# Output projection of a hybrid conv/attention layer: block products reordered, gate columns stored, x reloaded into other tiles

## The chip, the core and the metric

The kernel runs on one core of one Trainium2 chip. The metric is the device time of one launch in microseconds (us), as the median of several runs. Before the change it is 1453.81 us (three runs, 1452.35 to 1453.82).

## The reference, cut to what matters

One layer over a sequence of 512 positions and 2048 channels, in float32:

```python
mod = silu(c) @ w_ada + b_ada                     # shift, scale, gate: 2048 columns each
h = rms_norm(x, g_pre) * (1 + scale) + shift
p = h @ w_in                                      # cv, cg, cz, q, k, v, az, m_conv, m_attn
y_conv = conv_branch(cv, cg, cz, ...)             # ... @ w_conv_out
y_attn = attn_branch(q, k, v, az, ...)            # ... @ w_attn_out
merged = sigmoid(m_conv) * y_conv + sigmoid(m_attn) * y_attn
out = merged @ w_o                                # 512x2048 by 2048x2048: the output projection
x = x + gate * rms_norm(out, g_post)
```

## The kernel before, in words

Every float32 operand of a large matmul is kept as a sum of two float32r parts, high and low (`split`, L143: ScalarE casts the high part, VectorE subtracts it from the source to get the low one). `mm3` (L165) then makes one product from three matmuls: high by high, high by low, low by high. Weights arrive by `wraw` (L153, one DMA into a tile with tag "wr", three buffers) and are split by `wsplit` (L158, tags "wh" and "wl", three buffers each). All DMAs are issued from SyncE's queue (SP).

The stages in order of time: x is normalised and the convolution's input products run (to about 350 us), then attention and the depthwise convolution, the gates cz, ma and mc of the branches, the two branch projections (`gemm_y`: "ya" from w_attn_out, then "yc" from w_conv_out), and the output projection. The code is written with a planner: instructions are traced in program order, and a list scheduler puts each on its engine's queue by its own estimate of when operands and buffers are ready, earlier code first among the ready ones. It can issue an instruction long before its place in the code when a buffer is free. A tile's buffer is given to any later tile of its tag once all readers of the old one are done. `ordered` (L678) keeps the matmuls of the late stages in program order.

Tile pools that matter here: pages (`page`, 27 of 128x512), pairs (`pair_of`, 16 of 128x2x512), temps (`temp`, 12 of 128x512 in the late stages), "ws" (two of 128x2x512).

**Output projection.** It is done by a scheme of seven block products in place of eight (Winograd's form of Strassen's): the merged operand is cut into blocks B11, B21, B22 and the sums T1 to T4 (L988 to L994; B11 and T1 lie in the merged pairs mB[0..7], T2 and T3 in the pages mT23, T4 in mT4), the weights into a11, a21, a12, a22 and the sums s1 = a21 + a22 (L1067), s2 = s1 + a11 (L1070), s3 = a11 + a21 (L1079, in place of a21) and s4 = s2 + a12 (L1104, L1116). `G` walks over two halves of the output columns. In each half the first loop (t = 0 to 3, two of eight weight row blocks each) makes four products per t, each of 12 matmuls (`oprod`, L1001): in this order ox (s2 by T2), oz (a11 by B11), or (s3 by T3), oy (s1 by T1). In ox's turn both s2 sums are needed, and they are temps. After t = 3, q = oz - ox, ct = or - q and ct - oy are formed (L1076, L1078, L1084, L1087). The second loop adds a12 by B21 into oz, a22 by T4 into or and s4 by B22 into oy. For G = 1 it is cut in two: first all s4 products (L1111 to L1117), then a third loop over t (L1123) with the a22 and a12 products. There t = 0 and 1 run at once, and t = 2 and 3 are split and held (L1130), then run for row tile i = 0 and i = 1 one after the other (L1139), so that row tile 0 can be finished under the products of row tile 1.

`out_done` (L1025) squares a finished output block on ScalarE and multiplies it by the gate columns `gg[n]` on VectorE; `finish` (L1044) makes the reciprocal root of the sum of squares, adds x (L1052) and stores a row tile. x is read again by `x_again` (L1039) into a 1 MB tile of tag "wr", the tag of the weights' raw tiles.

**Gate columns.** `gate(n)` (L802) computes one quarter of gate times g_post, as a row copied over all partitions: 16 loads of w_ada rows (temps "adag"), a running sum on VectorE (L820), one matmul with ones, and L830/L831. gate(0) to gate(2) are worked in between the mc products, gate(3) between the ya products; `pump` draws one step or a few at each product. The result of gate(0) lies in `dist`, those of 1 to 3 each in a page from then to the end of the kernel.

Of the kernel before, what the change touches and what calls it, by code (L numbers as in the profile page):

```python
# [51 lines left out]
def hybrid_trunk(ctx: ExitStack, tc: tile.TileContext, x, c, w_ada, b_ada, g_pre, g_post, w_in,  # L52
# [17 lines left out]
    def page(name, dt=F32):  # L70
        return pp.tile([P, S], dt, tag="pg", name=name)
# [730 lines left out]
    def gate(n):  # L802
# [21 lines left out]
        gp = page(f"gg_{n}") if n else dist  # L824
# [7 lines left out]
        gg[n] = gp  # L832
# [206 lines left out]
    def x_again(t):  # L1039
        xr = wp.tile([P, 4, 512], F32, tag="wr", name=f"xr_{t}")  # L1040
        nc.sync.dma_start(out=xr.rearrange("p k n -> p (k n)"), in_=x2[t * P:(t + 1) * P, :])
        return xr

    def finish(t, xr, cuts=((0, 4),)):  # L1044
        z = small(1, f"fz_{t}")
        nc.vector.scalar_tensor_tensor(z, fss[:, 4 * t + 3:4 * t + 4], 1.0 / D, fz[:, t:t + 1],
                                       op0=ALU.mult, op1=ALU.add)
        r = rsqrt1(z, f"fr_{t}")
        for a, b in cuts:
            for n in range(a, b):  # L1050
                g = xr[:, n, :]
                nc.vector.scalar_tensor_tensor(g, og[t][n], r, g, op0=ALU.mult, op1=ALU.add)  # L1052
            nc.sync.dma_start(out=out2[t * P:(t + 1) * P, a * 512:b * 512],
                              in_=xr[:, a:b, :].rearrange("p k n -> p (k n)"))

    work.append(late_splits())
    for G in range(2):
# [3 lines left out]
        for t in range(4):  # L1061
            ra = wraw(w_o[0], 2 * t, 2, c0, 1024, f"oa_{G}_{t}")
            s1 = mp.tile([P, 2, S], F32, tag="ws", bufs=2, name=f"os1_{G}_{t}")
            nc.sync.dma_start(out=s1, in_=w_o[0].rearrange("(t p) n -> p t n", p=P)[:, KH + 2 * t:KH + 2 * t + 2,
                                                                                  c0 + S:c0 + 2 * S])
            a11, a21 = ra[:, :, :S], ra[:, :, S:]
            nc.vector.tensor_tensor(s1, a21, s1, op=ALU.add)  # L1067
            for k in range(2):
                s2[2 * t + k] = temp(f"os2_{G}_{2 * t + k}")
                nc.vector.tensor_tensor(s2[2 * t + k], s1[:, k, :], a11[:, k, :], op=ALU.add)  # L1070
            oprod(ox, wop_of(s2[2 * t:2 * t + 2], f"os2_{G}_{t}"), oT2, t, True)
            oprod(oz, wop(a11, f"oa11_{G}_{t}"), oB11, t, True)
            if t == 3:
                q = [temp(f"oq_{G}_{i}") for i in range(2)]
                for i in range(2):
                    nc.scalar.copy(q[i], oz[i])  # L1076
                for i in range(2):
                    nc.vector.tensor_tensor(q[i], q[i], ox[i], op=ALU.subtract)  # L1078
            nc.vector.tensor_tensor(a21, a11, a21, op=ALU.add)  # L1079
            oprod(orr, wop(a21, f"os3_{G}_{t}"), oT3, t, True)  # L1080
            if t == 3:
                ct = [temp(f"oc_{G}_{i}") for i in range(2)]
                for i in range(2):
                    nc.vector.tensor_tensor(ct[i], orr[i], q[i], op=ALU.subtract)  # L1084
            oprod(oy, wop(s1, f"os1_{G}_{t}"), oT1, t, True)
# [25 lines left out]
        for t in range(4):  # L1111
# [5 lines left out]
            oprod(oy, wop_of(s2[2 * t:2 * t + 2], f"os4_{G}_{t}"), oB22, t, False)  # L1117
        for t in (2, 3, 0, 1):
            for n in range(2):
# [3 lines left out]
        for t in range(4):  # L1123
# [8 lines left out]
            if t == 0:  # L1132
                for i in range(2):
# [4 lines left out]
                    finish(2 + i, x_again(2 + i))  # L1138
        for i in range(2):  # L1139
            xr = x_again(i)  # L1140
# [9 lines left out]
            finish(i, xr, ((0, 2), (2, 3), (3, 4)) if i else ((0, 4),))  # L1150
# [29 lines left out]
```

## Time and profile before

| | |
|---|---|
| median of the runs | 1453.81 us (1452.35 to 1453.82) |
| the profiled execution's own time | 1453.56 us |
| its span, first to last instruction | 1451.6 us |
| TensorE matmul busy (PE) | 1387.0 us, 96% |
| TensorE weight load busy (PEld) | 1176.7 us, 81% |
| VectorE busy (DVE) | 1175.2 us, 81% |
| ScalarE busy (ACT) | 558.8 us, 38% |
| mean DMA rate | 172 GB/s |
| mean granted TensorE clock | 0.986 of full speed |

All times of the trace are us from the start of its span. In a row of the timeline the first number is the start, the second the duration; in square brackets stands how long the engine was idle before the instruction, and what ended that. Matmuls are pipelined: a row shows 0.39 us for a 512-column matmul where the next one starts 0.227 us later, so a busy PE is not a PE at its peak; a product's length is best read from the starts of two successive products. SPq rows are the issue of a DMA; the data lands later. "PEclk" is the granted clock, 1.00 being 2.4 GHz.

### The profile page before, as it was taken

What the parts mean: (1) busy time and instruction counts of PE and PEld (TensorE: products, weight loads), DVE (VectorE), ACT (ScalarE), POOL (GpSimd) and SP (SyncE); (2) the same over time, 40 slices, a digit from 0 to 9 for tenths busy, and PEclk for the clock granted to TensorE, in tenths of its full rate; (3) what the DMA queues carried; (4) which work ended last, traced back from release to release, by engine and by line L of the source; (5) the groups of instructions that cost most, each with busy time, mean ns of one, the idle gap of its engine ahead of it and who ended that gap; (6) DMA issues with size and microseconds to landing.
All of it is one profiled execution on the core that took longest, in us unless ns stands there. A gap on an engine that the chain in (4) does not pass through costs nothing.

```text
span 1451.6 us, 20533 instructions
## 1 busy us (share of the span) xinstructions
PE 1387.0 (96%) x7903; PEld 1176.7 (81%) x7903; DVE 1175.2 (81%) x1916; ACT 558.8 (38%) x903; POOL 1.8 (0%) x8
## 2 busy tenths in 40 slices
PE   5999999999999999999999999999998999799995
PEld 4676788887778777789999999999986888688774
DVE  6997976988888886698987888899877758888786
ACT  3422232223443244444544444444436223344441
POOL 0000000000000000000000000000000000000000
PEclk9999999999999999999999999999999999999997
DMA  9888633332223223244645565666689633235455
GB/s 305 292 274 296 229 120 116 117 102 81 93 66 102 95 73 101 68 143 159 204 138 186 175 192 189 205 208 227 210 297 335 235 130 135 94 131 174 137 200 228
DMA packets 180323, 249.11 MB, mean 172 GB/s; under 512 B 9649, under 2 KB 120578, under 8 KB 179330
## 3 DMA queue, kind: packets, MB, share of 16 engines
q1 hardware_dynamic: 180226, 247.80, 51.2%
q8 instruction: 62, 1.02, 0.3%
q14 instruction: 35, 0.29, 0.1%
HBM read 218.41 MB, written 29.36 MB: 171 GB/s over the span
## 4 chain that ended last, share of the span: by engine, by line
PE 83%; DVE 9%; DMA 4%; ACT 1%; issue 1%; SPq 1%; DVEq 0%; ACTq 0%
PE pc L167 10%; PE pg_k L167 6%; PE py_yc L167 6%; PE pv L167 6%; PE py_ya L167 5%; PE pg_az L167 5%; PE pg_q L167 5%; PE x_ma L167 5%; PE x_mc L167 4%; PE z_ma L167 3%; PE y_ma L167 3%; PE y_mc L167 3%; PE z_mc L167 3%; PE x_cz L167 2%; PE oy L167 2%; PE oz L167 2%
## 5 line engine op out<-in xcount | busy, mean ns | idle before, releaser
L500 DVE SCALAR_TENSOR_TENSOR cacc<-u,cw,cacc 128x511 f32<-128x511 f32 (+14 forms) x240 | 164.3, 728 | 0.0
L167 PE MATMUL pc<-hp,wh_c 128*128 128x512 f32 x512 | 160.3, 398 | 2.6 <-DVE part L369 1.2
L167 PEld LDWEIGHTS pc<-hp,wh_c 128*128 128x128 f32 x512 | 95.9, 190 | 28.8 <-issue 2.7
L167 PE MATMUL pc<-hp,wl_c 128*128 128x512 f32 x256 | 99.2, 397 | 2.1 <-DVE wl_c L146 2.1
L167 PE MATMUL py_ya<-ya,wh_ya 128*128 128x512 f32 x256 | 80.5, 396 | 8.3 <-ACT wh_ya L145 8.3
L369 DVE TENSOR_TENSOR part<-pc,part 128x512 f32<-128x512 f32 x96 | 64.7, 687 | 24.1 <-PE pc L167 23.6
L167 PE MATMUL pv<-wh_v,hp 128*128 128x512 f32 x256 | 82.9, 397 | 0.9 <-DVE part L369 0.9
L167 PE MATMUL pg_q<-hp,wh_q 128*128 128x512 f32 x256 | 82.6, 398 | 0.0
L167 PE MATMUL pg_az<-hp,wh_az 128*128 128x512 f32 x256 | 81.4, 395 | 0.0
L167 PE MATMUL pg_k<-hp,wh_k 128*128 128x512 f32 x256 | 80.0, 392 | 0.0
L145 ACT CAST wh_c<-wr_c 128x1024 fp32r<-128x1024 f32 (+1 forms) x36 | 34.2, 956 | 103.7 <-DMA wr_c<-in_w_in_dram 49.7
L167 PEld LDWEIGHTS py_ya<-ya,wh_ya 128*128 128x128 f32 x256 | 48.8, 191 | 19.2 <-ACT wh_ya L145 8.7
L167 PEld LDWEIGHTS pc<-hp,wl_c 128*128 128x128 f32 x256 | 48.6, 191 | 14.1 <-DVE wl_c L146 3.3
L167 PEld LDWEIGHTS pv<-wh_v,hp 128*128 128x128 f32 x256 | 47.8, 188 | 14.3 <-issue 4.5
L167 PEld LDWEIGHTS pg_az<-hp,wh_az 128*128 128x128 f32 x256 | 47.7, 188 | 12.0 <-issue 2.7
L167 PEld LDWEIGHTS pg_q<-hp,wh_q 128*128 128x128 f32 x256 | 47.2, 188 | 12.3 <-issue 2.8
L167 PEld LDWEIGHTS pg_k<-hp,wh_k 128*128 128x128 f32 x256 | 47.9, 188 | 9.4
L307 DVE SCALAR_TENSOR_TENSOR acc<-ada,cact,acc 128x512 f32<-128x512 f32 (+1 forms) x52 | 50.5, 970 | 1.6 <-DMA ada<-in_w_ada_dram 1.4
L167 PE MATMUL pg_k<-hp,wl_k 128*128 128x512 f32 x128 | 51.0, 399 | 0.0
L167 PE MATMUL pv<-wl_v,hp 128*128 128x512 f32 x128 | 50.6, 395 | 0.0
L167 PE MATMUL pg_az<-hp,wl_az 128*128 128x512 f32 x128 | 50.5, 396 | 0.0
L167 PE MATMUL py_ya<-ya,wl_ya 128*128 128x512 f32 x128 | 50.5, 394 | 0.0
(399 smaller groups left out, 3944.1 us busy)
## 6 DMA issues: line engine op xcount, KB each, us to landing
ada<-in_w_ada_dram SPq DMA_DIRECT2D x128, 256.0 KB, 5.4
wr_ma<-in_w_in_dram SPq DMA_DIRECT2D x16, 1024.0 KB, 5.7
wr_mc<-in_w_in_dram SPq DMA_DIRECT2D x16, 1024.0 KB, 5.5
adag<-in_w_ada_dram SPq DMA_DIRECT2D x64, 256.0 KB, 5.7
wr_c<-in_w_in_dram SPq DMA_DIRECT2D x28, 512.0 KB, 6.0
wr_v<-in_w_in_dram SPq DMA_DIRECT2D x8, 1024.0 KB, 5.3
wr_q<-in_w_in_dram SPq DMA_DIRECT2D x8, 1024.0 KB, 5.1
wr_k<-in_w_in_dram SPq DMA_DIRECT2D x8, 1024.0 KB, 6.2
```

The costliest lines, as they stand in the source:

```text
L145: nc.scalar.copy(hi, src)
L167: mm = nc.tensor.matmul(ps, a[p], b[q], start=start and i == 0, stop=stop and i == 2, skip_group_check=more)
L307: nc.vector.scalar_tensor_tensor(acc, raw[:, kk - k0, :, :], cact[:, kk:kk + 1], acc, op0=ALU.mult, op1=ALU.add)
L369: nc.vector.tensor_tensor(part[i], ps[f], part[i], op=ALU.add)
L500: paced(nc.vector.scalar_tensor_tensor(cvo[t][:, s:], u[t][:, :S - s], wj, cvo[t][:, s:], op0=ALU.mult, op1=ALU.add))
```

## The change

Three things change. In `gate`, the columns for n = 1 to 3 are computed in a temp instead of a page and stored to DRAM scratch; ahead of the output projection three pages are allocated and the columns fetched back. `x_again` loads a row tile of x as two halves of 512 KB into two tiles of the pairs' pool instead of one 1 MB tile of tag "wr"; it is called for all four row tiles ahead of the third loop of G = 1, and `finish` stores each of them in halves (for row tile 1 as before, a half and two quarters). In the first loop of each G the order of the four products becomes oz, or, ox, oy (and for the very first t oz, oy, or, ox), with the sums moved to where they are first used; the sums after t = 3 stand in the function of the ox product.

```diff
--- before.py
+++ after.py
@@ -821,7 +821,7 @@
             yield
         bg = temp(f"bg_{n}")
         nc.sync.dma_start(out=bg, in_=b_ada2[2 * D + n * 512:2 * D + (n + 1) * 512].partition_broadcast(P))
-        gp = page(f"gg_{n}") if n else dist
+        gp = temp(f"gg_{n}") if n else dist
         nc.sync.dma_start(out=gp, in_=g_post[0][n * 512:(n + 1) * 512].partition_broadcast(P))
         yield
         pgt = gbank(f"pgt_{n}", "t")
@@ -829,7 +829,10 @@
         yield
         nc.vector.tensor_tensor(bg, pgt, bg, op=ALU.add)
         nc.vector.tensor_tensor(gp, gp, bg, op=ALU.mult)
-        gg[n] = gp
+        if n:
+            spill(f"gg{n}", gp)
+        else:
+            gg[0] = gp
         yield
 
     crs = []
@@ -1037,23 +1040,29 @@
         nc.vector.tensor_scalar(fz[:, t:t + 1], fz[:, t:t + 1], 1.0 / D, 4.0 * EPS, op0=ALU.mult, op1=ALU.add)
 
     def x_again(t):
-        xr = wp.tile([P, 4, 512], F32, tag="wr", name=f"xr_{t}")
-        nc.sync.dma_start(out=xr.rearrange("p k n -> p (k n)"), in_=x2[t * P:(t + 1) * P, :])
+        xr = []
+        for a in range(2):
+            xr.append(pair_of(f"xr_{t}_{a}", F32))
+            nc.sync.dma_start(out=xr[a].rearrange("p k n -> p (k n)"),
+                              in_=x2[t * P:(t + 1) * P, a * 1024:(a + 1) * 1024])
         return xr
 
-    def finish(t, xr, cuts=((0, 4),)):
+    def finish(t, xr, cuts=((0, 2), (2, 4))):
         z = small(1, f"fz_{t}")
         nc.vector.scalar_tensor_tensor(z, fss[:, 4 * t + 3:4 * t + 4], 1.0 / D, fz[:, t:t + 1],
                                        op0=ALU.mult, op1=ALU.add)
         r = rsqrt1(z, f"fr_{t}")
         for a, b in cuts:
             for n in range(a, b):
-                g = xr[:, n, :]
+                g = xr[n // 2][:, n % 2, :]
                 nc.vector.scalar_tensor_tensor(g, og[t][n], r, g, op0=ALU.mult, op1=ALU.add)
             nc.sync.dma_start(out=out2[t * P:(t + 1) * P, a * 512:b * 512],
-                              in_=xr[:, a:b, :].rearrange("p k n -> p (k n)"))
+                              in_=xr[a // 2][:, a % 2:a % 2 + b - a, :].rearrange("p k n -> p (k n)"))
 
     work.append(late_splits())
+    for n in range(1, 4):
+        gg[n] = page(f"gg_{n}")
+        fetch(f"gg{n}", gg[n])
     for G in range(2):
         c0 = G * 1024
         s2 = [None] * KH
@@ -1064,25 +1073,46 @@
             nc.sync.dma_start(out=s1, in_=w_o[0].rearrange("(t p) n -> p t n", p=P)[:, KH + 2 * t:KH + 2 * t + 2,
                                                                                   c0 + S:c0 + 2 * S])
             a11, a21 = ra[:, :, :S], ra[:, :, S:]
-            nc.vector.tensor_tensor(s1, a21, s1, op=ALU.add)
-            for k in range(2):
-                s2[2 * t + k] = temp(f"os2_{G}_{2 * t + k}")
-                nc.vector.tensor_tensor(s2[2 * t + k], s1[:, k, :], a11[:, k, :], op=ALU.add)
-            oprod(ox, wop_of(s2[2 * t:2 * t + 2], f"os2_{G}_{t}"), oT2, t, True)
-            oprod(oz, wop(a11, f"oa11_{G}_{t}"), oB11, t, True)
-            if t == 3:
-                q = [temp(f"oq_{G}_{i}") for i in range(2)]
-                for i in range(2):
-                    nc.scalar.copy(q[i], oz[i])
-                for i in range(2):
-                    nc.vector.tensor_tensor(q[i], q[i], ox[i], op=ALU.subtract)
-            nc.vector.tensor_tensor(a21, a11, a21, op=ALU.add)
-            oprod(orr, wop(a21, f"os3_{G}_{t}"), oT3, t, True)
-            if t == 3:
-                ct = [temp(f"oc_{G}_{i}") for i in range(2)]
-                for i in range(2):
-                    nc.vector.tensor_tensor(ct[i], orr[i], q[i], op=ALU.subtract)
-            oprod(oy, wop(s1, f"os1_{G}_{t}"), oT1, t, True)
+
+            def p1():
+                oprod(oz, wop(a11, f"oa11_{G}_{t}"), oB11, t, True)
+                if t == 3:
+                    for i in range(2):
+                        q[i] = temp(f"oq_{G}_{i}")
+                        nc.scalar.copy(q[i], oz[i])
+
+            def p5():
+                oprod(oy, wop(s1, f"os1_{G}_{t}"), oT1, t, True)
+
+            def p6():
+                for k in range(2):
+                    s2[2 * t + k] = temp(f"os2_{G}_{2 * t + k}")
+                    nc.vector.tensor_tensor(s2[2 * t + k], s1[:, k, :], a11[:, k, :], op=ALU.add)
+                oprod(ox, wop_of(s2[2 * t:2 * t + 2], f"os2_{G}_{t}"), oT2, t, True)
+                if t == 3:
+                    for i in range(2):
+                        nc.vector.tensor_tensor(q[i], q[i], ox[i], op=ALU.subtract)
+                    for i in range(2):
+                        ct[i] = temp(f"oc_{G}_{i}")
+                        nc.vector.tensor_tensor(ct[i], orr[i], q[i], op=ALU.subtract)
+
+            def p7():
+                nc.vector.tensor_tensor(s3, a11, a21, op=ALU.add)
+                oprod(orr, wop(s3, f"os3_{G}_{t}"), oT3, t, True)
+
+            q, ct, s3 = [None] * 2, [None] * 2, a21
+            if G == 0 and t == 0:
+                p1()
+                nc.vector.tensor_tensor(s1, a21, s1, op=ALU.add)
+                p5()
+                p7()
+                p6()
+            else:
+                p1()
+                nc.vector.tensor_tensor(s1, a21, s1, op=ALU.add)
+                p7()
+                p6()
+                p5()
         for i in range(2):
             nc.vector.tensor_tensor(ct[i], ct[i], oy[i], op=ALU.subtract)
             out_done(2 * G + 1, 2 + i, ct[i], ct[i], tmp(f"osq22_{G}_{i}"))
@@ -1115,7 +1145,9 @@
             for k in range(2):
                 nc.vector.tensor_tensor(s2[2 * t + k], s2[2 * t + k], a12[:, k, :], op=ALU.add)
             oprod(oy, wop_of(s2[2 * t:2 * t + 2], f"os4_{G}_{t}"), oB22, t, False)
+        xrs = [None] * NT
         for t in (2, 3, 0, 1):
+            xrs[t] = x_again(t)
             for n in range(2):
                 og[t][n] = page(f"ogf_{n}_{t}")
                 fetch(f"og_{n}_{t}", og[t][n])
@@ -1135,9 +1167,9 @@
                     nc.vector.tensor_tensor(g, oy[i], q[i], op=ALU.add)
                     out_done(2, 2 + i, g, g, temp(f"osq12_{G}_{i}"))
                     sums3(2 + i)
-                    finish(2 + i, x_again(2 + i))
+                    finish(2 + i, xrs[2 + i])
         for i in range(2):
-            xr = x_again(i)
+            xr = xrs[i]
             for t, w in held:
                 oprod(orr, w[0], oT4, t, False, (i,))
             g = temp(f"oc21_{G}_{i}")
@@ -1147,7 +1179,7 @@
             for t, w in held:
                 oprod(oz, w[1], oB21, t, False, (i,))
             out_done(2, i, oz[i], temp(f"oc11_{G}_{i}"), temp(f"osq11_{G}_{i}"))
-            finish(i, xr, ((0, 2), (2, 3), (3, 4)) if i else ((0, 4),))
+            finish(i, xr, ((0, 2), (2, 3), (3, 4)) if i else ((0, 2), (2, 4)))
 
 
 # ---- launch: one core; inputs and outputs as the reference has them ----
```

## Rows read from the trace of the kernel before

**Rows 1.** The page: busy time of each engine, its share, and instructions.

```profile
PE 1387.0 (96%) x7903; PEld 1176.7 (81%) x7903; DVE 1175.2 (81%) x1916; ACT 558.8 (38%) x903; POOL 1.8 (0%) x8
```

**Rows 2.** Busy time by stretch: length, PE, PEld, DVE, ACT, POOL, granted clock, DMA share, GB/s.

```profile
907.00:1074.00 167.00, 165.87 (x1371) 164.61 (x1370) 148.58 (x181) 72.49 (x91) 0.00 (x0) 1.00 0.66 219
...
1260.40:1268.10 7.70, 0.18 (x1) 0.00 (x0) 7.56 (x16) 3.13 (x6) 0.00 (x0) 0.81 0.00 0
1268.10:1281.50 13.40, 13.09 (x49) 10.38 (x50) 12.08 (x16) 7.71 (x11) 0.00 (x0) 0.85 0.36 117
1281.50:1346.60 65.10, 65.10 (x288) 53.70 (x286) 51.67 (x63) 28.81 (x42) 0.00 (x0) 1.00 0.45 155
1346.60:1354.90 8.30, 5.01 (x14) 3.74 (x14) 7.96 (x12) 4.28 (x8) 0.00 (x0) 0.79 0.41 131
...
1407.20:1440.40 33.20, 26.73 (x97) 19.81 (x96) 23.20 (x61) 9.85 (x21) 0.00 (x0) 0.90 0.59 222
1440.40:1451.60 11.20, 0.00 (x0) 0.00 (x0) 6.69 (x20) 0.67 (x2) 0.00 (x0) 0.60 0.48 187
```

**Rows 3.** Waits of TensorE from 1262 us on: total, times, longest.

```profile
PE ox L167 <- ACT wh_os L145: 9.6, 2, 7.5
...
PE or L167 <- ACT wh_oa L145: 3.3, 2, 3.0
```

**Rows 4.** Chain that ended last: a product of the output projection.

```profile
1281.46 2.72 PE ox L167 x12
```

**Rows 5.** Timeline around the start of the output projection.

```profile
1250.88 0.62 ACT L145 CAST mt23h<-mt 128x512 fp32r<-128x512 f32 x1 [4.28 <-PE py_yc L167]
...
1266.66 1.28 DVE L1070 TENSOR_TENSOR os<-os,wr_oa 128x512 f32<-128x512 f32 x2
1267.44 0.62 ACT L145 CAST wh_os<-os 128x512 fp32r<-128x512 f32 x1 [0.92 <-DVE os L1070]
...
1268.11 0.80 PE L167 MATMUL ox<-wh_os,mt23h 128*128 128x512 f32 x1 [7.52 <-ACT wh_os L145]
```

**Rows 6.** Timeline around the start of the second column half (G = 1).

```profile
1347.39 0.68 DVE L1070 TENSOR_TENSOR os<-os,wr_oa 128x512 f32<-128x512 f32 x1
...
1350.40 1.22 DVE L146 TENSOR_TENSOR wl_oa<-wr_oa,wh_oa 128x1024 fp32r<-128x1024 f32 x1
```

**Rows 7.** SP's queue and ScalarE, late in G = 1: loads of x and of raw weights.

```profile
1376.86 0.34 SPq L1041 DMA_DIRECT2D xr<-in_x_dram  x1
...
1407.13 0.38 SPq L155 DMA_DIRECT2D wr_ob<-in_w_o_dram  x1
...
1412.13 2.00 ACT L145 CAST wh_oa<-wr_ob 128x1024 fp32r<-128x1024 f32 x2 [3.06 <-DMA wr_ob<-in_w_o_dram]
1422.73 2.19 ACT L145 CAST wph_oa<-wr_ob 128x512 fp32r<-128x512 f32 x4 [8.60 <-DMA wr_ob<-in_w_o_dram]
1427.84 2.18 ACT L145 CAST wh_oa<-wr_ob 128x512 fp32r<-128x512 f32 x4 [2.92 <-DMA wr_ob<-in_w_o_dram]
```

**Rows 8.** VectorE: the finishing of row tiles 2 and 3, and the last one.

```profile
1411.57 1.41 DVE L1052 SCALAR_TENSOR_TENSOR xr<-ogf,fr_y,xr 128x512 f32<-128x512 f32 x2
...
1446.00 1.41 DVE L1052 SCALAR_TENSOR_TENSOR xr<-oc,fr_y,xr 128x512 f32<-128x512 f32 x2
```

**Rows 9.** Gate columns: their tile's rows, a later bias load, and loads of w_ada.

```profile
L825 SPq DMA_DIRECT2D gg<-in_g_post_dram x3: 328/382/572, 752.5 to 1137.9; - x3
L831 DVE TENSOR_TENSOR gg<-gg,bg x3: 682/691/691, 1027.2 to 1175.4; 128x512 f32<-128x512 f32 x3
...
1014.86 0.42 SPq L823 DMA_DIRECT2D bg<-in_b_ada_dram  x1
...
1039.47 3.12 SPq L809 DMA_DIRECT2D adag<-in_w_ada_dram  x4
```

**Rows 10.** DMA issues of the late stages: size and median us to landing.

```profile
xr<-in_x_dram SPq DMA_DIRECT2D x4, 1024.0 KB, 4.8
...
os<-in_w_o_dram SPq DMA_DIRECT2D x6, 512.0 KB, 3.8
```

## The prediction

> **What bounds the kernel now.** I read the page first: TensorE (PE) is busy 96% of the span, VectorE (DVE) 81% [rows 1], so what can be won lies where PE stands still or is slow. Next the busy time by stretch [rows 2]: from 907 to 1074 us PE is busy 165.87 of 167 us, but from 1260.4 us, where the branch projections end, three stretches stand out. In 1260.4 to 1268.1 PE does nothing, in 1346.6 to 1354.9 it is busy 5.0 of 8.3 us, in 1407.2 to 1440.4 it is busy 26.7 of 33.2, and in each the granted clock falls to between 0.79 and 0.90. The waits of PE name the culprits [rows 3]: ox on the cast of os (9.6 us), or on the cast of oa (3.3 us). What a product costs when nothing is late is read from the chain of waits: 2.72 us for its 12 matmuls [rows 4].
>
> The timeline tells why. At the start, ox is the first product, and its operand s2 is made at 1266.66 and cast at 1267.44 [rows 5]. DVE was busy 7.56 of the 7.7 us before [rows 2] with the last merged blocks, whose temps s2 also needs. ScalarE (ACT) meanwhile had idled 4.28 us before 1250.88 [rows 5]: a11 could have been cast then. At the start of G = 1 it is the same, s2 at 1347.39 [rows 6]. In the third loop it is another thing: the raw weights come late. x is loaded at 1376.86 into a tile of their tag, the next raw weights are issued only at 1407.13, and ACT waits 3.06, 8.60 and 2.92 us for such loads [rows 7].
>
> **The change, part by part.** A DVE subtraction over 128x1024 takes 1.22 us [rows 6], two over 128x512 1.28 us [rows 5].
>
> **A, the first t.** From the end of the branch projections at 1260.4 to t = 1 at 1281.46 [rows 2, 4] go 21.1 us; four products are 4 x 2.72 = 10.9, so 10.2 us are lost. After the change oz (a11 by B11) and oy (s1 by T1) come first; both need only weights and merged blocks made long before, so their splits can lie under the last branch projections, where ACT and DVE have gaps. They cover PE until 1260.4 + 5.4 = 1265.8. The third, or, takes a split buffer that the last branch projection holds to its end, so its low part stands behind DVE's chain, which ends at 1266.66 [rows 5]; with 1.22 us for it and 0.64 for one late split of T2/T3 it is there at 1268.5. So 2.7 us are lost still, and **7.5 us** gained. Bounds: 10.2 if DVE slips that split into its chain; 4.9 if it puts the s2 sums and their split (2 x 1.28) ahead.
>
> **B, the start of G = 1.** ox takes 8.3 us for 2.72 [rows 2]: 5.6 lost. Now oz leads, with a11 loaded and no temp needed, and or follows without one either; s2 is wanted 5.4 us later. But DVE is full there (7.96 of 8.3 us [rows 2]) with the outputs of G = 0, so I leave one subtraction, 1.2 us, and 0.4 for slow matmuls after it: 1.6 lost, **4.0 us** gained. Bounds: 5.6; and 2.8, if both first subtractions (2 x 1.22) stay uncovered.
>
> **C, the third loop.** Eight products are 21.8 us of the 33.2 [rows 2, 4]: 11.4 lost. x no longer stands in the weights' tag; its halves go into pairs mB[0..7], the first of which die after oy of t = 0 of G = 1, near 1354.9 + 3 x 2.72 = 1363 [rows 2, 4], far ahead of their use at 1411.57 [rows 8]. If such a load stands at the head of SP's queue before its pair is dead, the weights behind it wait too; they have a whole t, 10.9 us, to spare. So all raw weights of the third loop but the last can be there before 1407. Then DVE decides: it still has 23.20 + 6.69 = 29.9 us to do from 1407.2 to the end [rows 2]; it ended at 1447.4 [rows 8] and can't end before 1437.1, so at most 10.3 us come of the 11.4. The finishing of row tiles 2 and 3 stands ahead of the later splits in the code; it costs PE part of this. I take 2.4 us for two splits behind it (2 x 1.22): **7.9 us** gained. Lower bound 5.0: DVE does the whole finishing first, to 1411.57 as now and then four pairs of L1052, 4 x 1.41, to 1417.2 [rows 8]; PE has t = 0 done at 1412.6, and the next split is there at 1418.4: 5.8 lost, and 0.6 for one more split.
>
> **D, the end.** After the last matmul 11.2 us remain [rows 2], the same instructions as before for row tile 1: 0. Row tile 0 is stored in halves, the first earlier: between 0.7 less and 0.7 more (one L1052 either way, [rows 8]).
>
> **E, gate columns.** Three stores and three fetches of 256 KB; with four more loads for x in halves and three more stores of row tiles that makes 13 more issues on SP, at 0.34 us each [rows 7] 4.4 us, spread over stages in which SP mostly waits for buffers. Each new store waits for L831; behind it stand the next loads, which are issued ahead of need. That they free pages is worth little if they are fetched back early: the load for the first column tile was issued at 752.5, its use came at 1027.2 [rows 9], so the planner takes a free page as soon as it sees one. The temp they now take is held from load to store. 0, between 1.5 less (two pages for the conv branch ahead of the ya products) and 1.5 more (1.5 MB more traffic, at 219 GB/s for a DMA share of 0.66 [rows 2] 4.7 us of full transfer, of which a third may fall where PE waits for loads). x in halves: 512 KB lands in 3.8 us, 1 MB in 4.8 [rows 10], hidden by the 48 us that x has.
>
> **Sum.** 7.5 + 4.0 + 7.9 = 19.4 us. The profiled execution took 1453.56 us for its span of 1451.6, 0.25 below the median of the runs: 1453.56 - 19.4 = 1434.2, which I round to **1434**. All good bounds: 10.2 + 5.6 + 10.3 + 0.7 + 1.5 = 28.3, 1425.3. All bad ones: 4.9 + 2.8 + 5.0 - 0.7 - 1.5 = 10.5, 1443.1.
>
> **The rivals.** First, **VectorE's debt**. The change takes no work from DVE. Between 1268.1 and 1281.5 it is busy 12.08 of 13.4 us [rows 2]; if PE starts early and DVE can't, PE waits at t = 1 and 2 instead, and A shrinks to DVE's idle 1.3 us. With B, C and E at their bad bounds, 1.3 + 2.8 + 5.0 - 1.5 = 7.6 us, **1446**. Against it: in 1281.5 to 1346.6 DVE has 13.4 us of idle [rows 2], and in the third loop it idles 10.0 of 33.2, behind casts that wait for loads [rows 2, 7]. The Trainium skill, Perfetto Trace Analysis, section Identifying the Most-Contended Engine, judges VectorE by its occupancy and TensorE by the weight load's busy share, not the matmuls', and wants the most contended engine eased first. By that rule DVE (70% against 60% for PEld in the third loop) is the bound there, and a change that eases only PE's waits would give this rival's time.
>
> Second, **no change**: the planner already chooses by readiness, and if splits of the new first products land behind the same DVE chain while the weights' loads wait on the buffers of splits that DVE makes late, the stalls keep their length: 1453.6, within 2.9 us.
>
> Third, on the other side, **a temp too few**. The gate column's tile now stands in one of 12 temps, beside bias, running sum and w_ada rows, while the mc products need temps for every block. Loaded like the bias at 1014.86 and used at 1027.2 [rows 9], it holds one for 12.3 us at the least, and gate(2)'s as long at the end of mc. If a block's own temps wait behind both, PE waits 24.7 us, more than the 19.4 gained: 1434.2 + 24.7 = **1459**. It decides from 19.4 us of such waits on. Against it: w_ada rows are fetched four at a time ahead [rows 9], so temps are in reserve, and PE loses only 1.1 of 167 us in this stretch [rows 2].
>
> **How the numbers follow.** Forecast 0.70 (1425.3 to 1443.1), VectorE's debt 0.16 (1441 to 1450), no change 0.07, a temp too few 0.07. The range 1426 to 1447 holds nearly all of the forecast and two thirds of the debt, about 0.8. A measurement of this kernel can tell 0.2%, 2.9 us, from no change. Faster: 0.70 + 0.16 = 0.86; the same 0.07; slower 0.07.
>
> **What would show it.** A: the first matmul of oz within 1 us of the last py_yc, t = 1 starting some 13.5 us after it, not 21; wrong if PE waits there for the cast of oa. B: under 3 us lost where G = 1 starts, and no wait of ox on the cast of os. C: no wait of ACT on wr_ob beyond t = 3, and from the first oz or or of the third loop to the last matmul about 24 to 25 us, not 33. E: the same 167 us for the mc products, and the stop ahead of the ya products as long as before. The prediction is wrong if A and C show PE waiting for DVE as long as it waited for casts and loads.

## The result, and the profile after

The changed kernel takes 1438.32 us (median of four, 1437.18 to 1442.27) beside 1453.82 us for the kernel before on the same chip (four, 1452.35 to 1455.06): a ratio of 0.9899, 95% interval 0.9877 to 0.9920. That is 15.5 us less, where 19.4 were forecast. The profiled execution took 1437.88 us for a span of 1436.1. Its page, the answer to [rows 1], looks the same as before:

```profile
PE 1380.0 (96%) x7903; PEld 1171.2 (82%) x7903; DVE 1172.4 (82%) x1916; ACT 557.9 (39%) x903; POOL 1.8 (0%) x8
```

The gain is in the idle time, so it has to be read by stretch, as in [rows 2]. The columns are the same: stretch, length, PE, PEld, DVE, ACT, POOL, granted clock, DMA share, GB/s. The rows are the mc products, the ya products, the first t of the output projection, the rest of G = 0, the first loop of G = 1, its s4 products, its third loop, and the end.

```profile
907.40:1071.80 164.40, 163.73 (x1353) 162.32 (x1351) 147.41 (x179) 71.23 (x89) 0.00 (x0) 1.00 0.67 225
1071.80:1172.50 100.70, 91.39 (x389) 73.74 (x387) 61.73 (x82) 34.19 (x42) 0.00 (x0) 0.95 0.80 269
1260.00:1273.70 13.70, 11.89 (x50) 9.01 (x49) 13.24 (x22) 8.13 (x12) 0.00 (x0) 1.00 0.21 61
1273.70:1338.80 65.10, 65.10 (x288) 53.84 (x288) 55.93 (x70) 31.05 (x46) 0.00 (x0) 1.00 0.48 165
1338.80:1385.60 46.80, 44.45 (x193) 35.61 (x191) 35.61 (x47) 19.07 (x27) 0.00 (x0) 1.00 0.73 237
1385.60:1401.70 16.10, 13.12 (x49) 10.11 (x49) 12.08 (x21) 7.36 (x13) 0.00 (x0) 0.89 0.65 226
1401.70:1423.50 21.80, 21.80 (x97) 17.83 (x95) 20.57 (x61) 8.60 (x18) 0.00 (x0) 1.00 0.38 145
1423.50:1436.10 12.60, 0.15 (x1) 0.00 (x0) 7.84 (x22) 0.69 (x2) 0.00 (x0) 0.60 0.43 166
```

Three things strike. The stop of 7.7 us ahead of the projection and the 8.3 us at the start of G = 1 are gone: PE is busy 65.10 of 65.10 us up to the end of G = 0 and runs straight on. The third loop takes 21.8 us with PE never idle, where it took 33.2. But the first loop of G = 1 and the s4 products, which had lost next to nothing before, now lose about 2.9 and 5 us. The waits of PE from 1050 us on, the answer to [rows 3], name the new ones:

```profile
PE py_ya L167 <- ACT wh_ya L145: 9.0, 1, 9.0
PE ox L167 <- DVE wl_os L146: 2.8, 2, 2.3
PE oy L167 <- DVE wl_os L146: 2.8, 1, 2.8
PE ox L167 <- ACT wh_os L145: 1.1, 1, 1.1
```

The old culprits (9.6 us at ox for a cast of os, 3.3 at or for one of oa) are reduced to 1.1. The two waits on VectorE's split of os are new.

**The start**, the answer to [rows 5], in the timeline (start, duration, engine, line, operation; in brackets the idle time before it and what ended that):

```profile
1259.98 0.39 PE L167 MATMUL oz<-wh_oa,mgs 128*128 128x512 f32 x1
...
1261.14 1.22 DVE L146 TENSOR_TENSOR wl_os<-wr_oa,wh_os 128x1024 fp32r<-128x1024 f32 x1
...
1269.44 0.50 PE L167 MATMUL ox<-wh_os,mt23h 128*128 128x512 f32 x1 [1.14 <-ACT wh_os L145]
```

oz follows the last branch projection without a gap. The split for or slips into VectorE's chain at 1261.14, so what is left of the stop stands at ox, the last product of that t.

**Where the new waits come from.** SyncE's queue while G = 1 runs; each row is the issue of a load:

```profile
1359.71 1.70 SPq L1046 DMA_DIRECT2D xr<-in_x_dram  x2
...
1366.36 0.38 SPq L1143 DMA_DIRECT2D oa<-in_w_o_dram  x1
1370.59 0.34 SPq L1046 DMA_DIRECT2D xr<-in_x_dram  x1
1372.62 0.37 SPq L1143 DMA_DIRECT2D oa<-in_w_o_dram  x1
1373.08 0.42 SPq L1046 DMA_DIRECT2D xr<-in_x_dram  x1
...
1384.45 1.70 SPq L1046 DMA_DIRECT2D xr<-in_x_dram  x2
1387.13 0.38 SPq L1143 DMA_DIRECT2D oa<-in_w_o_dram  x1
1387.56 6.15 SPq L438 DMA_DIRECT2D ogf<-scratch_og  x8
```

The loads `oa` (L1143, L1113 before) bring the weight blocks a12 for s4. They have two tiles of tag "ws", which they share with the s1 blocks. x stands at the queue's head for its pairs, but what a block waits for last is its tile, as SyncE's waits from 1330 us on show:

```profile
SPq L1046 <- PE oy L167: 16.3, 7, 3.8
...
SPq L1143 <- DVE wl_os L146: 8.5, 2, 5.5
...
SPq L1143 <- DVE os L1146: 2.2, 2, 1.3
```

VectorE's queue shows what the blocks hold up:

```profile
1371.30 1.29 DVE L1146 TENSOR_TENSOR os<-os,oa 128x512 f32<-128x512 f32 x2 [2.47 <-DMA oa<-in_w_o_dram]
...
1373.64 1.29 DVE L1090 TENSOR_TENSOR os<-os,wr_oa 128x512 f32<-128x512 f32 x2
1378.50 0.69 DVE L1146 TENSOR_TENSOR os<-os,oa 128x512 f32<-128x512 f32 x1 [3.57 <-DMA oa<-in_w_o_dram]
...
1386.42 0.68 DVE L1146 TENSOR_TENSOR os<-os,oa 128x512 f32<-128x512 f32 x1
...
1393.40 0.69 DVE L1146 TENSOR_TENSOR os<-os,oa 128x512 f32<-128x512 f32 x1 [2.68 <-DMA oa<-in_w_o_dram]
```

The second block could be issued at 1372.62 only, when the addition at 1371.30 had read the first one out of its tile. It landed 5.9 us later, and until then VectorE stood at the addition of t = 1 (3.57 us), with the split that ox of t = 3 wants behind it: PE waited 2.26 us. The fourth block was issued at 1387.13, when the other half of that addition, which VectorE reached at 1386.42 only, had freed a tile. VectorE could read it 6.3 us later, at 1393.40; the split for s4 of t = 2 stood behind that addition, of t = 3, and PE waited 2.78 us.

**The ya products** take 2.2 us longer for another reason. SyncE's queue there:

```profile
1073.75 0.48 SPq L438 DMA_DIRECT2D ya<-scratch_yal  x1
1077.18 0.32 SPq L435 DMA_DIRECT2D scratch_gg<-gg  x1
1077.59 0.38 SPq L438 DMA_DIRECT2D ya<-scratch_yah  x1
...
1084.10 0.39 SPq L155 DMA_DIRECT2D wr_ya<-in_w_attn_out_dram  x1
```

The last of these rows in the kernel before:

```profile
1084.71 0.38 SPq L155 DMA_DIRECT2D wr_ya<-in_w_attn_out_dram  x1
```

VectorE in the changed kernel:

```profile
1076.46 0.69 DVE L831 TENSOR_TENSOR gg<-gg,bg 128x512 f32<-128x512 f32 x1 [2.21 <-DMA gg<-in_g_post_dram]
```

The store of the third gate column waits at the head of SyncE's queue for L831, which waits for a load. Behind it stand the last ya operands, the convolution's operands (cd) and the next raw weights of ya. Counted from the first ya product (1071.77 after, 1074.46 before) those weights are issued at 12.3 us, where it was 10.3, and PE goes on after its one long wait, for a cast of them, at 21.3 us, where it was 19.8. The other 0.7 of the 2.2 us go behind that wait.

**The account.** The profiled spans differ by 15.5 us. Stages are measured from starts of products: before the mc products, a part that the change leaves alone but for the place of two loads, the execution after is 2.1 us ahead; mc takes 0.6 less; ya 98.5 against 100.7, 2.2 more; yc the same 87.7; the projection to the end 191.0 against 176.0, 15.0 less. So from mc on the change gives 13.4 us, and 2.1 of the 15.5 are likely chance: in the profiles below the part ahead of mc varies by 5.7 us (905.6 to 911.3). I therefore compare stages, and whole times by their intervals.

### The profile page after: what moved, and what is told of

Read it like the earlier page. It is cut to its first block, busy times and chain, and to the rows that moved or that the text cites. A ratio compares the mean times of both kernels' runs of the same rounds, so it can differ in the third digit from the quotient of the medians.

```text
span 1436.1 us, 20551 instructions
## 1 busy us (share of the span) xinstructions
PE 1380.0 (96%) x7903; PEld 1171.2 (82%) x7903; DVE 1172.4 (82%) x1916; ACT 557.9 (39%) x903; POOL 1.8 (0%) x8
## 4 chain that ended last, share of the span: by engine, by line
PE 81%; DVE 9%; DMA 5%; issue 1%; ACT 1%; SPq 1%; DVEq 0%; ACTq 0%
PE pc L167 10%; PE py_ya L167 6%; PE pv L167 6%; PE pg_k L167 5%; PE pg_az L167 5%; PE pg_q L167 5%; PE x_ma L167 5%; PE py_yc L167 5%; PE x_mc L167 4%; PE z_ma L167 3%; PE y_ma L167 3%; PE y_mc L167 3%; PE z_mc L167 3%; PE x_cz L167 2%; PE or L167 2%; PE oz L167 2%
## 5 line engine op out<-in xcount | busy, mean ns | idle before, releaser
L167 PEld LDWEIGHTS py_ya<-ya,wh_ya 128*128 128x128 f32 x256 | 49.0, 192 | 21.1 <-ACT wh_ya L145 9.4
L167 PEld LDWEIGHTS pg_q<-hp,wh_q 128*128 128x128 f32 x256 | 47.2, 188 | 12.3 <-issue 2.8
```

What stands on the lines that cost most here:

```text
L167: mm = nc.tensor.matmul(ps, a[p], b[q], start=start and i == 0, stop=stop and i == 2, skip_group_check=more)
```

## The experiments

Three theories on the new waits. **Slots** (1): a12 has two tiles, so each block is loaded when an earlier one is read. **x** (2): the moved loads of x stand ahead of a12 in SyncE's queue (2a) and share the DMA engines with it (2b). **VectorE behind** (3): PE, no longer held up, simply overtakes VectorE. And one on the gate: the store's place in the queue. Each ratio is to runs of the kernel before on the same chip (medians 1452.8 to 1453.9). The table has what each profile shows, in us: the ya products; the first t, from the last branch projection on; t = 1 to 3 of the first loop of G = 1 up to oy of t = 3 (11 x 2.72 = 29.9 when nothing is late); oy of t = 3 with the four s4 products (13.6); the third loop (21.9); the end; and the whole projection.

| kernel | time | ratio to before | ya | first t | t 1-3 | s4 | third | end | projection |
|---|---|---|---|---|---|---|---|---|---|
| before | 1453.8 | 1 | 98.5 | 20.7 | 29.9 | 14.4 | 33.1 | 11.3 | 191.0 |
| after | 1438.3 | 0.9899 (0.9877 to 0.9920) | 100.7 | 13.4 | 32.9 | 18.9 | 21.9 | 12.5 | 176.0 |
| after again | 1440.5 | 0.9910 (0.9895 to 0.9925) | 100.2 | 14.4 | 32.2 | 20.3 | 21.9 | 12.5 | 178.1 |
| order alone | 1442.6 | 0.9933 (0.9919 to 0.9947) | 98.4 | 13.4 | 31.9 | 14.1 | 33.1 | 11.3 | 180.3 |
| x alone | 1447.4 | 0.9960 (0.9947 to 0.9973) | 97.7 | 20.7 | 29.9 | 17.8 | 21.9 | 12.5 | 184.5 |
| gate alone | 1456.4 | 1.0022 (1.0012 to 1.0031) | 100.9 | 21.1 | 29.9 | 14.7 | 33.1 | 11.5 | 192.0 |
| no gate | 1436.7 | 0.9883 (0.9868 to 0.9897) | 99.4 | 13.6 | 31.6 | 17.7 | 21.9 | 12.3 | 173.6 |
| x in its own queue | 1440.9 | 0.9913 (0.9893 to 0.9932) | 101.2 | 13.4 | 36.3 | 14.1 | 21.9 | 12.4 | 174.5 |
| a12 in pairs | 1435.6 | 0.9873 (0.9853 to 0.9893) | 100.8 | 13.5 | 30.3 | 14.1 | 21.9 | 12.7 | 168.9 |
| additions behind | 1440.2 | 0.9906 (0.9887 to 0.9926) | 100.9 | 14.4 | 29.9 | 18.0 | 23.0 | 12.2 | 174.2 |
| common first t | 1441.7 | 0.9913 (0.9888 to 0.9938) | 100.2 | 14.7 | 31.7 | 20.3 | 21.9 | 12.5 | 177.5 |
| gate column 2 in a page | 1438.4 | 0.9891 (0.9874 to 0.9907) | 97.1 | 14.5 | 32.2 | 20.3 | 21.9 | 12.4 | 178.2 |
| pairs, no gate | 1432.0 | 0.9856 (0.9840 to 0.9873) | 97.8 | 13.5 | 30.3 | 14.1 | 21.9 | 12.6 | 168.8 |

### The parts alone

Order alone: the hunk of the product order on the kernel before.

> The kernel before with the new order of the products alone (gate columns in pages, x in the weights' tiles as before). Theory 1 (slots): the two new waits of the changed kernel, 2.3 us at ox of t = 3 of G = 1 and 2.8 us at the s4 products, come of VectorE standing at an s4 addition for a weight block that is late because it has only two buffers of tag ws; x has no part in it. Then both waits are here too, the start of the projection and of G = 1 gain 7.4 + 5.6 us, the two loops of G = 1 give back up to 7.7, the third loop loses its 11.4 us as before: about 1448 us, 0.996 of before. Rival, theory 2 (x): the weight blocks are late because the loads of x stand ahead of them in SyncE's queue and share the DMA engines with them. Then neither wait is here, and all 13 us stay: about 1441 us, 0.991.

Both theories are half right. The s4 products take 14.1 us, as before: the new order alone doesn't bring their wait. At t = 3 of G = 1, 2.0 us are still lost. VectorE's waits there, and the DMA share (last but one column) of the ten us in which the first two blocks are loaded, first of this kernel, then of the changed one:

```profile
DVE os L1137 <- DMA oa<-in_w_o_dram: 3.9, 2, 2.4
```

```profile
1366.00:1376.00 10.00, 10.00 (x46) 8.27 (x45) 4.61 (x6) 3.29 (x4) 0.00 (x0) 1.00 0.34 107
```

```profile
1366.00:1376.00 10.00, 10.00 (x46) 8.28 (x45) 5.19 (x7) 4.02 (x6) 0.00 (x0) 1.00 0.70 234
```

With the same two slots but half the traffic, VectorE can read the second block 3.5 us after its issue (1372.00 to 1375.53) instead of 5.9. A slow landing is not the whole of it, though: the fourth block takes 6.6 us here, without any wait of PE, since it is issued 41.2 us after the start of G = 1 and not 48.3. The third loop is untouched at 33.1 us: of the change's parts, x alone is what it needs.

x alone: the hunks of `x_again`, `finish` and their calls on the kernel before.

> The kernel before with x loaded into the merged pairs alone. Both theories: the third loop of G = 1 loses its waits on raw weights, 11.4 us, and the end gets up to 1.4 us longer, since VectorE becomes the bound there. Theory 1 (slots): nothing new in the first two loops of G = 1: about 1444 us, 0.993 of before. Theory 2 (x): the s4 products wait for their weight blocks behind x by 4 to 8 us: 1448 to 1452 us, 0.996 to 0.999. If it gives less than the 11.4 us without a wait at s4, the new order itself is needed for the gain in the third loop.

The third loop has its full gain without the new order, the end is 1.3 us longer, and the s4 products lose 3.4 us more than before. The time, 1447.4 us, lies just under what theory x had forecast (1448 to 1452); slots had 1444. PE's wait at s4 is a different one here, for VectorE's subtraction ct - oy:

```profile
PE oy L167 <- DVE oc L1090: 2.3, 1, 2.3
```

VectorE had stood 3.74 and 1.90 us at two additions for a12 blocks before it.

Gate alone, and the changed kernel without it.

```diff
-        gp = page(f"gg_{n}") if n else dist
+        gp = temp(f"gg_{n}") if n else dist
...
+        if n:
+            spill(f"gg{n}", gp)
...
```

> The kernel before with the gate columns stored and fetched alone. Theory: the store of the last gate column stands in SyncE's queue ahead of the fetches for the ya products and waits for VectorE, so the stop ahead of ya gets 1 to 2.3 us longer and nothing else changes: 1454.8 to 1456 us, 1.001 to 1.0015 of before. Rival: the pages that it frees let the convolution's operands be fetched earlier and pay for that: within 1 us of before.

> The changed kernel without the gate columns' part (columns kept in pages, no stores and fetches). Theory: the stop ahead of ya is as short as in the kernel before and the rest is as in the changed kernel: 1.7 us less than the changed kernel's 1438.3, about 1436.6, 0.988 of before. Rival: the three pages that the columns then hold are missed in the output projection (late fetches of finished outputs, a late third loop): 1438 or more.

The gate's part costs 3.2 us by itself (0.12 to 0.31%), a little more than expected; in the profile 2.4 us are lost in ya and 1.0 in the projection, and nothing pays for it. Without it the changed kernel takes the time expected, 1436.7, though its interval overlaps that of the whole change, and the parts are not those expected: ya is 1.3 us shorter, not 2.2, and the projection, which was to stay as it was, is 2.4 us shorter.

### What makes the weight blocks late

x in its own queue:

```diff
-            nc.sync.dma_start(out=xr[a].rearrange("p k n -> p (k n)"),
+            nc.gpsimd.dma_start(out=xr[a].rearrange("p k n -> p (k n)"),
```

> The changed kernel with the eight loads of x issued from GpSimd's queue (idle there) instead of SyncE's; same tiles, same bytes. Theory 2a (head of the queue): a load of x that waits for its pair to die keeps the weight blocks of s4 behind it in SyncE's queue; with x in a queue of its own they are issued as soon as their slots are free, VectorE's waits for them shrink to those of the kernel with the new order alone, the s4 products take 14 us instead of 18.9 and ox of t = 3 about 4 instead of 5.7: 3 to 6 us less than the changed kernel, about 1434. Theory 2b (shared DMA engines): x moves the same bytes at the same time, so the weight blocks land as late as now: ox 5.7 and s4 18 to 19 us again, 1438. Theory 1 (two slots) gives the same as 2b.

The s4 products are as quick as 2a says, but ox of t = 3 is later than ever, and the time, 1440.9 us, is neither theory's. VectorE there:

```profile
1383.49 1.29 DVE L1146 TENSOR_TENSOR os<-os,oa 128x512 f32<-128x512 f32 x2 [5.05 <-DMA oa<-in_w_o_dram]
1384.70 1.29 DVE L1090 TENSOR_TENSOR os<-os,wr_oa 128x512 f32<-128x512 f32 x2
```

The second block again waits for the first one's tile and lands beside x, 6.1 us by the trace. This time the planner has put the s2 sums (L1090) behind that addition too, so PE waits 4.23 us for a cast. The head of SyncE's queue is not the cause at t = 3, and another queue doesn't take x off the DMA engines. The Trainium skill says so of these two kinds of queue (DMA: Bandwidth & Descriptors, section SWDGE vs HWDGE vs iDMA): both feed the same 16 engines, which take turns between them. The landing times agree, 6.1 us here against 5.9 with x in SyncE's queue. How much of the quick s4 products is owed to the free queue, and how much to PE's being 4 us later, this run can't say. A third thing differs as well. VectorE makes both halves of the addition of t = 1 in one go here (x2 at 1383.49), as it does with the new order alone:

```profile
1375.53 1.29 DVE L1137 TENSOR_TENSOR os<-os,oa 128x512 f32<-128x512 f32 x2 [2.42 <-DMA oa<-in_w_o_dram]
```

In the changed kernel the planner has put the second half 8 us behind the first (1378.50 and 1386.42). That half frees the tile of the fourth block, which is issued 48.3 us after the start of G = 1; here it is 45.0, with the order alone 41.2, and in both the s4 products are quick. So the wait at s4 may come from the planner's order on VectorE as much as from x; no run separates them.

a12 in pairs:

```diff
-            a12 = mp.tile([P, 2, S], F32, tag="ws", bufs=2, name=f"oa12_{t}")
+            a12 = pair_of(f"oa12_{t}", F32)
```

> The changed kernel with the weight blocks of s4 of G = 1 loaded into dead pairs, ahead of x, instead of the two tiles of tag ws. If late weight blocks are the whole cause of the two waits, ox of t = 3 takes 2.7 instead of 5.7 us and the s4 products with oy 13.6 to 14.5 instead of 18.9: 7 to 8 us less than the changed kernel, about 1431. Rival, theory 3 (the new order leaves VectorE behind PE whatever is loaded): the 2 us that the kernel with the new order alone loses at t = 3 stay, or come back elsewhere in G = 1: 4 to 6 us less, about 1433. If the last part is VectorE's work alone, the third loop or the end gets longer by what the loops gain: 1436 or more.

Both waits are gone, the third loop and the end hardly change, and the projection takes 168.9 us, 7.1 and 9.2 less than in the two profiles of the changed kernel. In the medians 3 to 5 us of that show, the intervals overlap, and 1435.6 us misses the forecast of 1431: it is the stages that decide between the theories. Counted from the start of G = 1 the blocks are issued 17 to 27 us earlier, all before any x, and VectorE waits for none of them any more (its waits in G = 1 up to the third loop, whole list):

```profile
1351.54 1.73 SPq L1143 DMA_DIRECT2D oa<-in_w_o_dram  x2
...
1361.82 0.96 SPq L1143 DMA_DIRECT2D oa<-in_w_o_dram  x2
1363.78 0.34 SPq L1046 DMA_DIRECT2D xr<-in_x_dram  x1
```

```profile
DVE wl_os L146 <- ACT wh_os L145: 3.3, 2, 3.1
DVE os L1112 <- DMA os<-in_w_o_dram: 2.9, 2, 1.8
DVE wl_oa L146 <- ACT wh_oa L145: 2.1, 2, 1.5
```

So late blocks are nearly the whole of it, and VectorE isn't behind by its work: only 0.4 us of the 2.0 that order alone lost at t = 3 are left. x moves the same bytes here, and the two blocks whose landing the trace has still take 3.9 and 6.8 us; it is the slots that turn such times into waits. The edit takes x's head start away as well: a12 gets the first dead pairs, and the first load of x is issued 22 us after the start of G = 1 instead of 10. The Trainium skill's Perfetto Trace Analysis, section Optimization Strategy, says that the same gap repeating on the engine that should be saturated can mean too little room for the next tile, in the number of buffers for one. VectorE's three waits for oa (2.47, 3.57, 2.68 us) look like that, though on an engine that isn't the one to saturate.

Additions behind (a token keeps two of VectorE's s4 additions behind a split):

```diff
+                if t % 2:
+                    tc.stamp_issue_order_token(i.ins, {1: "s4a", 3: "s4b"}[t])
...
```

> The changed kernel with two of the four s4 additions held behind a split on VectorE's queue: that of t = 1 behind ox's split of t = 3, that of t = 3 behind the split of s4 of t = 2. The loads stay where they are. If VectorE's place in the queue is what turns a late load into a wait of PE, ox of t = 3 takes 3 us instead of 5.7; but the slots are freed later, so the s4 products are no faster, 18 to 21 us: between 2 us less and 1 us more than the changed kernel, 1436 to 1439. Rival: the additions stand there because nothing else is to be done, PE waits as long as now at both places: 1438.

The stop at ox is gone (29.9), the s4 products are no better (18.0), and the third loop is 1.1 us longer, 0.8 of it a wait for a split. The time, 1440.2 us, is over its forecast of 1436 to 1439. The order on VectorE that was tried decides where PE meets the late block, not whether.

Common first t (the first t in the order of all others):

> The changed kernel with the first t of all in the common order oz, or, ox, oy instead of oz, oy, or, ox. If the start is bound by VectorE's chain behind the last branch projection (s2 and its split end some 10 us after it in either order), ox comes one product earlier and waits one product longer, 2.7 us: t = 1 begins 16 us after the last branch projection, not 13.7, and the time is 1440 to 1441. Rival: VectorE does the sums earlier since they are wanted earlier, and the start is the same: 1438.

Not settled. The time, 1441.7 us, is 0.7 over its forecast, and not by its reason: the first t takes 14.7 us, and with the special order it took 13.4 to 14.5 in nine profiles. That order is worth 1.3 us at the most, not 2.7; the rest of the time lies in the s4 products, 20.3 us as in the repeat below.

### Repeat, and the repair

> The changed kernel once more, beside the two below on the same chip. If its two new waits are a matter of the queues and not of one execution, the profile shows them again: ox of t = 3 of G = 1 over 4.5 us, the s4 products with oy 17 to 20 us, the output projection 176 us from the last branch projection to the end. Rival: they were chance, and one of the two is under 1 us.

Both waits are there again: 2.3 and 6.7 us lost, the second a little more than expected.

Gate column 2 in a page:

```diff
-        gp = temp(f"gg_{n}") if n else dist
+        gp = (page if n == 2 else temp)(f"gg_{n}") if n else dist
...
```

> The changed kernel with the third gate column (n = 2) kept in a page; the other two are stored and fetched as in the change. Theory: the store of that one column is what stands ahead of the fetches for ya, so the ya products take 98 to 99 us instead of 100.7 and the output projection stays as it is: 1.5 to 2.5 us less than the changed kernel, 1436. Rival: the stores and fetches as such cost, whichever they are, through the DMA engines: a third of the effect, 1437.5 or more.

The one store accounts for the loss ahead of ya: 97.1 us against 100.2 in the changed kernel beside it. The median is 2.0 us lower, though the intervals overlap; the stage carries the reading, for in the thirteen profiles ya takes 97.1 to 99.4 us without that store and 100.2 to 101.2 with it. PE's wait, 9.0 and 9.6 in the two profiles of the changed kernel:

```profile
PE py_ya L167 <- ACT wh_ya L145: 6.5, 1, 6.5
```

Pairs, no gate: both repairs together.

> The changed kernel with the weight blocks of s4 in dead pairs and without the gate columns' part. The two costs found lie in different stages and should add: 7 us in the loops of G = 1 and 2 us ahead of ya, 1429 to 1430, 0.984 of before. Rival: the columns kept in pages make the fetches of the finished outputs late, or the last part is VectorE's alone: no more than 7 us, 1431 or more.

1432.0 us, 8.4 less than the changed kernel on the same chip, and the intervals (0.9840 to 0.9873, 0.9895 to 0.9925) stand apart. The stages add as expected (97.8 and 168.8). The whole is 2 to 3 us above the forecast and within the rival's 1431 or more, but the rival's reasons aren't seen: the third loop and the end take 21.9 and 12.6 us, as in the changed kernel. Of the new stops, this remains of the first loop and the s4 products:

```profile
1338.00:1382.00 44.00, 43.92 (x192) 35.70 (x191) 37.78 (x50) 19.82 (x30) 0.00 (x0) 1.00 0.74 251
1382.00:1396.00 14.00, 13.81 (x61) 11.17 (x60) 11.91 (x22) 8.04 (x15) 0.00 (x0) 1.00 0.83 272
```

## Why the prediction was right or wrong

The sum had 19.4 us, the medians differ by 15.5. The three parts that it forecast gave more than it said, with the end 22.4 us; two costs that it had at nothing took 7.3 and 2.2 away; and 2.7 lie ahead of ya, 2.1 of them likely chance. That the total comes so near is in part luck, by errors that cancel.

**A, the first t: the size right, the place wrong.** 7.3 us gained for 7.5 (20.7 to 13.4). The agreement is luck: not or but ox waits, since the split for or did slip into VectorE's chain, as the upper bound had it, and s2 then came late behind it.

**B, the start of G = 1: right in kind, too small.** No stop is left, 5.1 us gained for 4.0. The subtraction that I left uncovered was covered, by two products of PE.

**C, the third loop: right in kind, too small.** Its third loop was to take 24 to 25 us and takes 21.9; 11.2 us gained for 7.9. ScalarE waits for no raw weights there. The planner laid the splits into the small operations of the finishing instead of behind them. The bound that VectorE's work sets came true one stretch later: the end is 1.2 us longer. The last product of oz is done at 1423.65, but its output is taken up only behind the finishing of row tile 0:

```profile
1425.09 1.41 DVE L1058 SCALAR_TENSOR_TENSOR xr<-oc,fr_y,xr 128x512 f32<-128x512 f32 x2
...
1426.42 0.68 DVE L1032 TENSOR_TENSOR oc<-oz,gg 128x512 f32<-128x512 f32 x1
```

Third loop and end together give 10.0 us; the bound worked out from VectorE's 29.9 us was 10.3. **D**, forecast as 0 within 0.7, is this 1.2.

**What the sum missed.** The step that failed is the one on what x does to the loads behind it, in C: "they have a whole t, 10.9 us, to spare". It holds for the raw weights of the third loop. It was not asked of the other weights in that queue, the a12 blocks, which have no t to spare: they have two tiles and are loaded one as the other is read. VectorE, standing at an addition for such a block, keeps back splits that PE wants. Price in the profiled execution: 2.9 us at t = 3 and 4.4 at the s4 products, 7.3 in all. It is not x's alone: at t = 3 the new order by itself loses 2.0 us, a term that A and B had at nothing, and with the moved loads of x in SyncE's queue five profiles lose 1.7 to 2.9 there, so x adds little, though the second block lands later; the 4.4 at s4 came with the order and the moved loads together, through a fourth block issued late, and whether by x or by the planner's order on VectorE stays open. Without these waits the projection gives 22.2 us (191.0 to 168.8 us with both repairs), more than the whole forecast.

**E, gate columns: wrong size.** Forecast 0 within 1.5; it costs 2.2 us ahead of ya here and 3.2 alone. I wrote that behind each store stand "the next loads, which are issued ahead of need". Ahead of ya they aren't: PE stands still there until the raw weights have landed and are cast. That the freed pages are worth little held: the columns are fetched back some 45 us ahead of the projection, and no stage is shorter by them.

**The rivals.** No change and a temp too few did not come: mc took 164.4 us. VectorE's debt came in another shape. PE does wait for VectorE's splits now, but VectorE stands idle then, for a load. The prediction gave this rival, priced at 1446 us from rows, the support of a rule of the Trainium skill (Perfetto Trace Analysis, section Identifying the Most-Contended Engine): the most contended engine is the one with the highest occupancy, and it is to be eased first. VectorE's work was left as it was and the time fell to 1438; the trace agrees with the rule only in the third loop and the end, where VectorE is busy 20.57 of 21.80 us and the output waits for it.

## What to carry to other kernels

Before a load is moved forward in a queue, list all loads behind it and ask each how many tiles it has and what stands behind its first reader: here the raw weights had a whole t and the a12 blocks nothing. Here a wait of VectorE for a load cost PE, which needed the next split, though VectorE was busy only 12.08 of the 16.10 us; the cure was a dead tile for the late load, which let it be issued early, while another queue and another order on VectorE only moved the wait. A store that waits for its data should not stand ahead of the fetches with which a stage begins.

## What I had not expected of the hardware

A stop can cost more than the wait. The second one, 2.78 us, was followed by a lower granted clock (columns as above; the clock is the third number from the right):

```profile
1385.60:1392.00 6.40, 6.17 (x26) 4.54 (x25) 5.11 (x9) 3.08 (x7) 0.00 (x0) 1.00 0.75 229
1392.00:1394.70 2.70, 0.00 (x0) 0.00 (x0) 1.30 (x3) 0.50 (x1) 0.00 (x0) 1.00 1.04 399
1394.70:1401.70 7.00, 6.96 (x23) 5.57 (x24) 5.66 (x10) 3.77 (x6) 0.00 (x0) 0.76 0.41 156
```

In the 7 us after it the mean is 0.76 of 2.4 GHz, so the products run at the lower level, 1.2 GHz, for part of it: of the 5.3 us that oy of t = 3 and the s4 products lost in all, 3.0 are waits. The wait of 2.26 us at ox was followed by no such loss (2.9 us in all, clock 1.00 in the 3.0 us after it). While PE stood still for the second, the DMA engines moved 399 GB/s at a share of 1.04: the eight fetches of finished outputs are issued from 0.4 us behind that block on. How much of its 6.3 us is theirs no run shows.
